# An encoder layer on one core: the FFN norm's factors on its rows instead of on the gate/up weights, other row pairs turned on TensorE, p evictions by load

## The chip, the cores and the metric

One NeuronCore of a Trainium2 chip runs one program. The metric is the device time of one execution in microseconds, from the first to the last instruction with what lies around it, and the median of several runs of a kernel. Engines: PE is TensorE's matmul, PEld its weight load, DVE is VectorE, ACT is ScalarE, POOL is GpSimd, SP issues the DMAs.

## The reference

One layer over x (2048 rows of 1024) mixes the rows with a gated delta net and an RG-LRU, and then computes the FFN and the per-layer embedding; the parts around the change are these:

```python
r = r + jnp.concatenate([dn_out, lru_out], axis=-1) @ w_out[i]
h2 = rmsnorm(r, norm2_g[i])            # r * rsqrt(mean(r*r) + eps) * norm2_g
gate = dwconv(h2 @ ffn_wg[i], ffn_conv_w[i], FFN_CONV_LEFT) + ffn_conv_b[i]
r = r + (jax.nn.gelu(gate) * (h2 @ ffn_wu[i])) @ ffn_wd[i]
pg = jax.nn.sigmoid(rmsnorm(r, ple_norm_g[i]) @ ple_wg[i] + ple_bg[i])
r = r + pg * (p[i] @ ple_wp[i])
return rmsnorm(r, final_g)
```

Everything is float32; D is 1024, D_FF 2816 (22 blocks of 128), and the FFN's convolution has three taps along the rows.

## The kernel before

**Numbers.** Each float32 operand of a large product is split into two float16 parts, high and low, by a ScalarE copy to float16 and a VectorE subtraction (split, L1668: copies L1673 and L1677, subtractions L1675 and L1679), and a product is the sum of three float16 products. Before a split, an operand is scaled by a power of two, worked out from the sum of its squares: ScalarE squares with an accumulated sum, one matmul with a matrix of ones adds over the partitions (for the gate/up weights L1859), and pow2_scale (L391) makes the scale and its inverse in six small VectorE steps.

**The FFN's products** use Strassen's scheme with seven products instead of eight over two halves each of rows, inner dimension and columns. operands (L1681) makes the seven operands of a side from four blocks: three are blocks themselves, four are sums or differences that GpSimd makes in place (L1702). product (L1706) issues one of the seven products in the matmuls of L1723, twelve of 512 columns each for a gate/up product. Products share banks: product 6 adds to the bank of product 1 and starts only after that was evicted (AFTER). gu_unit (L1884) is one unit: a gate (even n) or an up (odd n) projection of two column blocks for half of the rows (u is 0 or 1). units (L1727) interleaves two units in the order 1, 3 and 7 of the last, 2, 5, 4 of the last, 6. Products 1, 6, 5, 4 are evicted by ScalarE (L1927), products 2, 3, 7 by a VectorE addition (L1932). room (L1907) says which buffer an eviction must wait for: in an up projection with u = 1 it is the one that the first gate tile's convolution frees.

**One turn of the FFN** is a j from 0 to 10, four units. Beside the products stand: pair_weights (L1823), which loads the weights of a projection to come, multiplies them in place by norm2_g on GpSimd (L1851), squares them (L1854, summed at L1856), and splits their seven operands; gate_tile (L1963), which waits for the gate's products and for the act buffers, and makes tap scales (L1974), the middle tap on ScalarE (L1977), two side taps on VectorE (L1979, L1981) and the gelu (L1985); mult (L1988), which multiplies by the up projection on GpSimd (L1995); and act_post (L2000), which squares, scales and splits the result into seven operands, in sums of 128x1024 on GpSimd (L1702), stores them in DRAM and frees the act buffers for the next turn's gate_tile.

**The FFN norm.** norm_pairs (L1750) takes the rows in eight pairs of 128-row tiles, as the second output projection (out_lru, matmuls in L452, additions to r in L1580) finishes them in the order of TILES. Of each pair it squares the rows (L1769), makes the inverse root on VectorE, copies the rows times this factor on ScalarE into hv (L1777), stores r in DRAM (L1781), and makes the seven right operands. Pairs 0, 2, 4, 6 make and split them and turn the halves with seven DMA transposes (L1805); pairs 1, 3, 5, 7 turn the four blocks first, with 16 TensorE transposes (turned, L635) and four ScalarE evictions (L1794), and split into place. Pairs 0 to 3 serve the units with u = 0, pairs 4 to 7 those with u = 1.

**p.** p_products (L2384) multiplies p by ple_wp between FFN and down projection (matmuls in L452). Its post evicts the half m = 1 of each tile on VectorE (L2401) and m = 0 on ScalarE (L2404).

**What sets the order.** No engine's queue is ordered by the chip: a planner in the kernel (Sched, L158) runs before compilation. Each stream of work is a Python generator that yields steps with a modelled cost per engine (st), waits for named events (W) and takes memory from one arena (M). run (L250) always issues the step that can start earliest by the model, plus 20 ns for each unit of its stream's priority (PR, L53; a small number goes first), and memory is given in order of priority. So each changed cost, step or priority can move instructions anywhere behind it. S.t holds the modelled time up to which each engine is taken.

Of the kernel before, what the change touches and what calls it, by code (L numbers as in the profile page):

```python
# [25 lines left out]
PAGE = 4 * KB  # L26
SPOT, LX, LD = 0, 0, 0
AFTER_SUM = 5000
# [23 lines left out]
PARTS = (0, 1)  # L52
PR = {'main': 6, 'quarter': 5, 'build': 0, 'ring': 3, 'wo': 2, 'last': 0, 'norm': 2, 'lx': 2, 'conv': 2, 'dn': 2, 'prep': 2, 'chain': 6, 'z': 3, 'post': 2, 'lru': 1, 'lruout': 4, 'op': 2, 'pw': 3, 'evac': 0, 'cat': 5}  # L53

# [297 lines left out]
class Kern:  # L352
# [172 lines left out]
    def wprep(self, key, src, nk, n, gain, place, pieces=1, after=None, fold=False):  # L525
# [50 lines left out]
        if pieces > 1:  # L576
            yield st(dve=80)
            nc.vector.tensor_reduce(sm[:, 0:1], sm[:, 8 : 8 + (nk if fold else pieces)], axis=AX.X, op=ALU.add)
            tot = sm[:, 0:1]
        b = yield st(pe=20, bank=1, lag=SPOT)  # L580
        spot = self.bank(b)[:, 0:1]
# [429 lines left out]
    def head_post(self, h, which, G):  # L1011
# [45 lines left out]
        if which == "k":  # L1057
            bufs = yield M(2 * KB, 2 * KB)
            for q in range(4):
                sl = av[:, q * 512 : q * 512 + 512].rearrange("p (t n) -> p t n", t=4)  # L1060
                yield st(dve=c_tt(512))
                nc.vector.tensor_tensor(sl, sl, st_[:, 16 + 4 * q : 20 + 4 * q, None].to_broadcast([128, 4, 128]), op=ALU.mult)
                yield ahead(730)
                nc.sync.dma_start(dst[:, 4 * q : 4 * q + 4, 2], sl)
                b = yield st(pe=4 * 110, bank=1)
                P = self.bank(b)
                for i in range(4):
                    nc.tensor.transpose(P[:, i * 128 : i * 128 + 128], sl[:, i], c["ident"])
                kt = bufs[q % 2]
                yield st(act=c_act(512))  # L1070
                nc.scalar.activation(kt.f32(512), P, AF.Copy)
                S.release(b)
                yield st(dma=730)
                nc.sync.dma_start(dst[:, 4 * q : 4 * q + 4, 0], kt.f32(4, 128))
            for x in bufs:
                x.free()
# [673 lines left out]
    def norm_pairs(self):  # L1750


        nc, S = self.nc, self.S
        yield W("r", TILES[0], 1)
        sb = yield M(*[2 * KB] * 4, high=True)
# [3 lines left out]
        def begin(i):  # L1759
# [15 lines left out]
            for k, t in enumerate(ts):  # L1775
                yield st(act=c_act(D, 1))
                nc.scalar.activation(hv[:, k], self.rt(t), AF.Copy, scale=y[:, k : k + 1])  # L1777
            smb.free()
# [9 lines left out]
            v = [hv[:, k, z * 512 : z * 512 + 512] for z in range(2) for k in range(2)]  # L1788
            if i % 2:
                for x in v:  # L1790
                    b = yield st(pe=4 * 160, bank=1)
                    P = self.turned(x, b)
                    yield st(act=c_act(512))
                    nc.scalar.activation(x, P, AF.Copy)  # L1794
                    S.release(b)

            def put(n, x):
                if i % 2:
                    to = self.hU[u][n].f16(8, 512)[:, :, o : o + 128]
                    yield from self.split(x.rearrange("p (a n) -> p a n", n=128), to[:, 0:4], to[:, 4:8], 512)  # L1800
                    return
# [12 lines left out]
            if not left[0]:  # L1814
                S.fire("h2", 1)
                for x in sb:
                    x.free()
# [5 lines left out]
    def pair_weights(self):  # L1823
# [3 lines left out]
        for n in range(22):  # L1827
# [21 lines left out]
            for i in range(2):  # L1849
                yield st(pool=c_pool(1024) * 0.8)  # L1850
                nc.gpsimd.tensor_tensor(v[i], v[i], c["g2"][:, :, None].to_broadcast([128, KT, 128]), op=ALU.mult)  # L1851
            for i in range(2):
                yield st(act=c_act(1024))
                nc.scalar.activation(self.junk.b16(KT, 128), v[i], AF.Square, accum_out=sm[:, 8 + i : 9 + i])  # L1854
# [5 lines left out]
            yield from self.pow2_scale(spot, 1, 16384.0, w.s, w.inv, sm[:, 4:6])  # L1860
            S.release(b)
            blocks = [v[i][:, z * 4 : z * 4 + 4] for i in range(2) for z in range(2)]

# [520 lines left out]
    def p_products(self):  # L2384
# [12 lines left out]
        def post(t, m, b):  # L2397
            j, u = yield from ring.take()
            if m:
                yield st(dve=c_stt(512))  # L2400
# [228 lines left out]
    def go(self):  # L2629
# [13 lines left out]
        S.spawn(self.setup(), 0)  # L2643
        g1, g2 = (lambda: c["g1"]), (lambda: c["g2"])
        base = dict(k=4, q=0, v=8, z=12, lx=16, lg=20)
# [19 lines left out]
PACK = [  # L2665
    ("g1", 8), ("g2", 8), ("g3", 8), ("qkvw", 48), ("lxw", 16), ("lxb", 4), ("ba", 8), ("bx", 8),
    ("lam", 8), ("gl", 4), ("gd", 4), ("alog", 8), ("dtb", 8), ("fcw", 66), ("fcb", 22),
# [3 lines left out]
    "x", "p", "pack", "w_in", "w_ba", "w_gate", "w_out", "w_gu", "w_d", "ple_wg", "ple_wp",  # L2671
    "ple_bg", "final_g",
]


def lay_out(a):
# [13 lines left out]
    def all_rows(v):  # L2690
        return np.broadcast_to(np.asarray(v).reshape(1, -1), (128, np.asarray(v).size))

    parts = dict(
        g1=flat(rows(a["norm1_g"][0])), g2=flat(rows(a["norm2_g"][0])), g3=flat(rows(a["ple_norm_g"][0])),
        qkvw=flat(rows(a["dn_conv_w"][0]).transpose(0, 2, 1)), lxw=flat(rows(a["lru_conv_w"][0]).transpose(0, 2, 1)),
# [15 lines left out]
    for i, n in enumerate(("lru_wa", "lru_wx")):  # L2711
# [10 lines left out]
        ple_wg=np.asarray(a["ple_wg"])[0], ple_wp=np.asarray(a["ple_wp"])[0],  # L2722
        ple_bg=np.asarray(a["ple_bg"]), final_g=np.asarray(a["final_g"]).reshape(1, D),
    )

# [46 lines left out]
```

## Time and profile before

| | us |
|---|---|
| median of 3 runs (lowest, highest) | 2797.17 (2789.87, 2801.34) |
| the profiled execution | 2788.9 |
| its span, first to last instruction | 2787.2 |
| TensorE busy in the span | 2575.5 |
| VectorE, ScalarE, GpSimd busy | 1858.1, 1490.4, 928.3 |
| mean granted clock of TensorE | 0.973 |

Busy times count an engine's instructions from start to end. A row of a timeline gives the start, the length and the line of a run of like instructions, with the idle time before it and what ended it in brackets. A row of waits gives who waited for whom: in total, how often, and the longest. The granted clock is a share of full speed.

### The profile page before, as it was taken

To read this page: it belongs to the slowest core of one execution; us is meant where nothing else is said; L and a number is where in the kernel's file an instruction comes from. 1 tells how busy PE (TensorE), PEld (TensorE's weight loads), DVE (VectorE), ACT (ScalarE), POOL (GpSimd) and SP (SyncE) were. 2 spreads that over 40 slices of the span, in tenths; PEclk is the share of its full clock that TensorE was granted. 3 is DMA by queue.
4 is the path that set the end of the run, shared out by engine and by line. 5 is a ranking of instruction groups with operands and counts; after the bars stand their busy time and mean duration, and the time that the engine had idled before them with its cause. 6 is when DMAs were issued, how large, how long until landed. Compare 5 with 4: busy or idle time off the path is not lost. (4 is left out here: it accounts for less than half of the span.)

```text
span 2787.2 us, 40376 instructions
## 1 busy us (share of the span) xinstructions
PE 2575.5 (92%) x14072; PEld 1313.2 (47%) x14072; DVE 1858.1 (67%) x3861; ACT 1490.4 (53%) x3120; POOL 928.3 (33%) x662
## 2 busy tenths in 40 slices
PE   7998997999889989988999999999997799999998
PEld 4454453556565665443444444444443344444443
DVE  8668967976885667587666767776668842222458
ACT  6576767575657764366565665665656510101323
POOL 1133534745230000135555556555555500000000
PEclk9999999999999999998999999999999999999999
DMA  5232252366453477564222233323326754457973
GB/s 193 72 102 61 67 142 67 94 189 204 129 168 116 126 256 260 131 170 103 87 87 90 71 92 102 99 84 102 102 59 198 258 179 144 160 166 226 275 188 143
DMA packets 433452, 387.68 MB, mean 139 GB/s; under 512 B 158688, under 2 KB 362464, under 8 KB 433248
## 3 DMA queue, kind: packets, MB, share of 16 engines
q1 hardware_dynamic: 433248, 385.10, 46.6%
q8 instruction: 111, 1.82, 0.3%
q14 instruction: 93, 0.76, 0.1%
HBM read 229.82 MB, written 128.97 MB: 129 GB/s over the span
## 5 line engine op out<-in xcount | busy, mean ns | idle before, releaser
L1723 PE MATMUL P<-arena 128*128 128x512 f16 x5166 | 1139.4, 383 | 41.3 <-ACT arena L1927 39.7
L452 PE MATMUL P<-arena 128*128 128x512 f16 x4224 | 988.6, 385 | 26.2 <-DVE arena L2401 9.3
L1723 PEld LDWEIGHTS <-arena 128*128 128x128 f16 x5166 | 509.9, 99 | 659.9 <-issue 68.3
L452 PEld LDWEIGHTS <-arena 128*128 128x128 f16 x4224 | 414.5, 100 | 482.5 <-issue 48.0
L1702 POOL TENSOR_TENSOR arena<-arena 128x512 f32<-128x512 f32 (+1 forms) x200 | 373.5, 1872 | 357.7 <-DVE arena L1679 254.7
L1679 DVE SCALAR_TENSOR_TENSOR arena<-arena 128x512 f16<-128x512 f32 (+2 forms) x408 | 433.1, 1099 | 76.1 <-ACT arena L1677 75.1
L1677 ACT ACTIVATE arena<-arena 128x512 f16<-128x512 f32 (+2 forms) x408 | 281.4, 722 | 261.0 <-POOL arena L1702 127.3
L2186 DVE SCALAR_TENSOR_TENSOR arena<-P,arena 128x512 f32<-128x512 f32 x95 | 70.2, 749 | 214.7 <-PE P L1723 189.1
L1995 POOL TENSOR_TENSOR arena<-arena 128x512 f32<-128x512 f32 x88 | 129.1, 1486 | 128.4 <-ACT arena L1985 81.6
L1932 DVE TENSOR_TENSOR arena<-P,arena 128x512 f32<-128x512 f32 x132 | 90.6, 687 | 117.3 <-PE P L1723 115.0
L1851 POOL TENSOR_TENSOR arena<-arena 128x1024 f32<-128x1024 f32 x44 | 91.9, 2091 | 200.6 <-DMA arena<-in_w_gu_dram 200.6
L1927 ACT ACTIVATE arena<-P 128x512 f32<-128x512 f32 x176 | 102.5, 589 | 97.8 <-PE P L1723 91.8
L734 DVE SCALAR_TENSOR_TENSOR arena<-P,arena 128x511 f32<-128x511 f32 (+1 forms) x192 | 140.5, 742 | 1.9
L2237 ACT ACTIVATE arena<-arena 128x1024 bf16<-128x1024 f32 x16 | 16.9, 1057 | 231.9 <-DVE arena L2186 222.1
L1257 POOL TENSOR_TENSOR arena<-arena 128x512 f32<-128x512 f32 x64 | 118.3, 1866 | 57.7 <-DVE arena L1207 45.8
L553 POOL TENSOR_TENSOR arena<-arena 128x1024 f32<-128x1024 f32 (+1 forms) x25 | 52.1, 2090 | 195.8 <-DMA arena<-in_w_in_dram 195.7
L1455 ACT ACTIVATE arena<-P,arena 128x128 f32<-128x128 f32 x128 | 46.8, 365 | 98.7 <-PE P L1449 64.7
L1466 DVE SCALAR_TENSOR_TENSOR arena<-arena,P 128x128 f32<-128x128 f32 x128 | 43.7, 343 | 54.0 <-PE P L1461 19.9
L2110 ACT ACTIVATE arena<-arena 128x256 bf16<-128x256 f32 x88 | 35.9, 408 | 77.2 <-DMA arena<-in_w_d_dram 76.9
L1460 PE MATMUL P<-arena 128*128 128x128 f32 x256 | 60.3, 318 | 18.0 <-ACT arena L1458 9.6
L1160 POOL TENSOR_TENSOR arena<-arena 128x512 f32<-128x512 f32 x32 | 41.0, 1280 | 104.6 <-DVE arena L1157 95.9
L1444 DVE SCALAR_TENSOR_TENSOR arena<-P,arena 128x128 f32<-128x128 f32 x128 | 44.3, 347 | 44.3 <-PE P L1442 42.9
(240 smaller groups left out, 3487.1 us busy)
## 6 DMA issues: line engine op xcount, KB each, us to landing
arena<-hd SPq DMA_DIRECT2D x160, 256.0 KB, 3.3
actd<-arena SPq DMA_DIRECT2D x148, 256.0 KB, 2.6
arena<-actd SPq DMA_DIRECT2D x49, 640.0 KB, 4.0
arena<-in_w_gu_dram SPq DMA_DIRECT2D x44, 512.0 KB, 4.3
arena<-in_x_dram SPq DMA_DIRECT2D x32, 512.0 KB, 7.1
at<-arena SPq DMA_DIRECT2D x64, 256.0 KB, 2.8
arena<-at SPq DMA_DIRECT2D x128, 128.0 KB, 3.3
rd<-arena SPq DMA_DIRECT2D x32, 512.0 KB, 3.3
```

What stands on the lines that cost most here:

```text
L452: self.nc.tensor.matmul(out, l, r, start=(i + j == 0), stop=(i + j == m - 1))
L734: nc.vector.scalar_tensor_tensor(a[:, lo:hi], P[:, lo - sh : hi - sh], tp[:, j : j + 1], a[:, lo:hi], op0=ALU.mult, op1=ALU.add)
L1257: nc.gpsimd.tensor_tensor(pv[:, i % 2], a(slice(2 * i, 2 * i + 2)), b(slice(2 * i, 2 * i + 2)), op=ALU.mult)
L1677: nc.scalar.activation(hi, x, AF.Copy, scale=scale)
L1679: nc.vector.scalar_tensor_tensor(lo, x, scale, hi, op0=ALU.mult, op1=ALU.subtract)
L1702: nc.gpsimd.tensor_tensor(v[at], v[p], v[q], op=ALU.add if plus else ALU.subtract)
L1723: self.nc.tensor.matmul(out, l, r, start=(p in (1, 2, 5) and i + j == 0), stop=(p in (2, 3, 4) and i + j == m - 1), skip_group_check=True)
L1851: nc.gpsimd.tensor_tensor(v[i], v[i], c["g2"][:, :, None].to_broadcast([128, KT, 128]), op=ALU.mult)
L1927: nc.scalar.activation(d, P, AF.Copy)
L1932: nc.vector.tensor_tensor(d, P, d, op=ALU.add)
L1995: nc.gpsimd.tensor_tensor(v, v, U.buf.f32(2, 2, 4, 128)[:, i, s], op=ALU.mult)
L2186: nc.vector.scalar_tensor_tensor(v, self.bank(b), self.dsm[:, at : at + 1], v, op0=ALU.mult, op1=ALU.add)
```

## The change

The gain norm2_g leaves the gate/up weights: pair_weights no longer multiplies them on GpSimd. Instead norm_pairs loads norm2_g once as a row over all partitions, scales it by a power of two, and each row of hv is made by one VectorE instruction that multiplies by the row's factor and by that row; the scale's inverse goes into the weights' inverse scale. TensorE turns the pairs 4 to 7 instead of 1, 3, 5 and 7. The eviction of p's products goes to VectorE when the planner has VectorE free earlier than ScalarE, and else to ScalarE. The priority numbers of 'lx' and 'wo' rise from 2 to 4 and from 2 to 3. The lags that are written in (SPOT, KL, H2L) are all 0. norm2_g leaves the packed constants and becomes an input of its own.

```diff
-PR = {'main': 6, 'quarter': 5, 'build': 0, 'ring': 3, 'wo': 2, 'last': 0, 'norm': 2, 'lx': 2, 'conv': 2, 'dn': 2, 'prep': 2, 'chain': 6, 'z': 3, 'post': 2, 'lru': 1, 'lruout': 4, 'op': 2, 'pw': 3, 'evac': 0, 'cat': 5}
+PR = {'main': 6, 'quarter': 5, 'build': 0, 'ring': 3, 'wo': 3, 'last': 0, 'norm': 2, 'lx': 4, 'conv': 2, 'dn': 2, 'prep': 2, 'chain': 6, 'z': 3, 'post': 2, 'lru': 1, 'lruout': 4, 'op': 2, 'pw': 3, 'evac': 0, 'cat': 5}
...
     def norm_pairs(self):
...
+        (gb,) = yield M(4 * KB)
+        g = gb.f32(D)
+        yield st(dma=1456)
+        nc.sync.dma_start(g, self.io["norm2_g"].partition_broadcast(128))
+        gs = self.A.alloc(64).f32(16)
+        self.ginv = gs[:, 2:3]
+        yield st(act=c_act(D))
+        nc.scalar.activation(self.junk.b16(D), g, AF.Square, accum_out=gs[:, 0:1])
+        yield from self.pow2_scale(gs[:, 0:1], 1, 1.0, gs[:, 1:2], self.ginv, gs[:, 4:6])
+        yield st(dve=c_tt(D))
+        nc.vector.tensor_scalar(g, g, gs[:, 1:2], None, op0=ALU.mult)
+        S.fire("g2")
         yield W("r", TILES[0], 1)
...
             for k, t in enumerate(ts):
-                yield st(act=c_act(D, 1))
-                nc.scalar.activation(hv[:, k], self.rt(t), AF.Copy, scale=y[:, k : k + 1])
+                yield st(dve=c_stt(D))
+                nc.vector.scalar_tensor_tensor(hv[:, k], self.rt(t), y[:, k : k + 1], g, op0=ALU.mult, op1=ALU.mult)
...
-            if i % 2:
+            if i >= 4:
                 for x in v:
-                    b = yield st(pe=4 * 160, bank=1)
+                    b = yield st(pe=4 * 160, bank=1, lag=H2L)
                     P = self.turned(x, b)
...
             def put(n, x):
-                if i % 2:
+                if i >= 4:
...
-                for x in sb:
+                for x in sb + [gb]:
                     x.free()
...
     def pair_weights(self):
...
-            for i in range(2):
-                yield st(pool=c_pool(1024) * 0.8)
-                nc.gpsimd.tensor_tensor(v[i], v[i], c["g2"][:, :, None].to_broadcast([128, KT, 128]), op=ALU.mult)
             for i in range(2):
                 yield st(act=c_act(1024))
                 nc.scalar.activation(self.junk.b16(KT, 128), v[i], AF.Square, accum_out=sm[:, 8 + i : 9 + i])
...
             yield from self.pow2_scale(spot, 1, 16384.0, w.s, w.inv, sm[:, 4:6])
             S.release(b)
+            yield W("g2")
+            yield st(dve=75)
+            nc.vector.tensor_tensor(w.inv, w.inv, self.ginv, op=ALU.mult)
...
     def p_products(self):
...
         def post(t, m, b):
             j, u = yield from ring.take()
-            if m:
+            if S.t["dve"] < S.t["act"]:
                 yield st(dve=c_stt(512))
...
```

## Rows read from the trace of the kernel before

**Rows 1.** Stretches: PE, PEld, DVE, ACT, POOL busy; clock; DMA share; GB/s.

```profile
0.00:1130.00 1130.00, 1022.04 (x6971) 608.72 (x6972) 835.91 (x2210) 734.42 (x1835) 336.96 (x330) 0.97 0.47 141
1130.00:1300.00 170.00, 142.74 (x656) 68.04 (x655) 126.39 (x267) 94.22 (x166) 65.70 (x41) 0.92 0.59 141
...
1480.00:2090.00 610.00, 582.61 (x2664) 263.80 (x2662) 421.03 (x534) 367.85 (x653) 346.81 (x187) 0.98 0.29 89
2090.00:2250.00 160.00, 125.99 (x528) 53.69 (x527) 127.34 (x146) 85.16 (x125) 78.59 (x48) 0.91 0.66 211
```

**Rows 2.** Waits of PE, 1480 to 2100 us: total, times, longest.

```profile
PE P L1723 <- ACT arena L1927: 27.4, 8, 3.4
```

**Rows 3.** Timeline of PE, 1300 to 2260 us: start, length, line, [idle before].

```profile
1563.27 24.73 PE L1723 MATMUL P<-arena 128*128 128x512 f16 x106 [3.42 <-ACT arena L1927]
...
1623.07 14.84 PE L1723 MATMUL P<-arena 128*128 128x512 f16 x68
...
1797.46 23.04 PE L1723 MATMUL P<-arena 128*128 128x512 f16 x106 [3.43 <-ACT arena L1927]
```

**Rows 4.** Stretch right behind the wait; columns as in rows 1.

```profile
1563.27:1567.00 3.73, 3.73 (x10) 1.41 (x10) 3.73 (x4) 3.73 (x3) 1.42 (x1) 0.54 0.00 0
```

**Rows 5.** Timeline of DVE in that turn.

```profile
1627.59 0.69 DVE L1932 TENSOR_TENSOR arena<-P,arena 128x512 f32<-128x512 f32 x1 [0.67 <-PE P L1723]
1628.20 0.35 DVE L1974 TENSOR_SCALAR arena<-arena 128x3 f32<-128x3 f32 x2
...
1630.79 6.54 DVE L1979 SCALAR_TENSOR_TENSOR arena<-arena 128x2047 f32<-128x2047 f32 x2
```

**Rows 6.** Timeline of ACT in that turn.

```profile
1638.48 0.72 ACT L1677 ACTIVATE arena<-arena 128x512 f16<-128x512 f32 x1 [2.55 <-POOL arena L1702]
...
1640.69 1.08 ACT L1927 ACTIVATE arena<-P 128x512 f32<-128x512 f32 x2 [0.61 <-DVE arena L1981]
```

**Rows 7.** Timeline of POOL in that turn.

```profile
1605.34 2.35 POOL L1702 TENSOR_TENSOR arena<-arena 128x1024 f32<-128x1024 f32 x1 [4.82 <-DVE arena L1679]
1607.64 1.90 POOL L1851 TENSOR_TENSOR arena<-arena 128x1024 f32<-128x1024 f32 x1
...
1611.80 2.36 POOL L1851 TENSOR_TENSOR arena<-arena 128x1024 f32<-128x1024 f32 x1
1614.12 5.56 POOL L1702 TENSOR_TENSOR arena<-arena 128x1024 f32<-128x1024 f32 x2
1629.28 9.17 POOL L1702 TENSOR_TENSOR arena<-arena 128x512 f32<-128x512 f32 x4 [9.60 <-DVE arena L1679]
```

**Rows 8.** Single lines: times run, duration ns min/median/max, forms.

```profile
L1777 ACT ACTIVATE arena<-arena x16: 1131/1140/1150, 1174.1 to 1260.5; 128x1024 f32<-128x1024 f32 x16
...
L2518 DVE SCALAR_TENSOR_TENSOR arena<-arena x16: 1275/1284/1286, 2709.6 to 2782.2; 128x1024 f32<-128x1024 f32 x16
...
L1805 SPq DMA_TRANSPOSE arena<-arena x28: 1232/1276/2403, 1180.4 to 1276.8; - x28
...
L1856 DVE TENSOR_TENSOR arena<-arena x22: 148/160/2312, 1155.9 to 2050.4; 128x1 f32<-128x1 f32 x22
...
L1702 POOL TENSOR_TENSOR arena<-arena x200: 1261/1680/3195, 1167.2 to 2234.9; 128x512 f32<-128x512 f32 x80, 128x1024 f32<-128x1024 f32 x20
...
L2401 DVE TENSOR_SCALAR arena<-P,arena x16: 727/740/751, 2145.0 to 2206.0; 128x512 f32<-128x512 f32 x16
```

**Rows 9.** Waits of PE, 1130 to 1300 us.

```profile
PE P L635 <- ACT arena L1777: 17.8, 4, 10.0
```

**Rows 10.** Timeline of PE around the FFN norm.

```profile
1222.42 1.12 PE L635 MATMUL P<-arena 128*128 128x128 f32 x4 [5.85 <-ACT arena L1777]
...
1263.49 2.77 PE L1723 MATMUL P<-arena 128*128 128x512 f16 x6
```

**Rows 11.** Waits of PE, 2090 to 2250 us.

```profile
PE P L452 <- DVE arena L2401: 9.3, 2, 6.8
...
PE P L452 <- ACT arena L2404: 3.9, 4, 1.3
```

More of the change, by code (lines that the diff above doesn't have):

```diff
@@ L26 @@
 PAGE = 4 * KB
-SPOT, LX, LD = 0, 0, 0
+SPOT = 0
+KL = 0
+H2L = 0
+LX, LD = 0, 0
 AFTER_SUM = 5000
@@ L579, in wprep @@
             tot = sm[:, 0:1]
-        b = yield st(pe=20, bank=1, lag=SPOT)
+        b = yield st(pe=20, bank=1, lag=SPOT if ("xT", 3) in S.ev else 0)
         spot = self.bank(b)[:, 0:1]
@@ L1064, in head_post @@
                 nc.sync.dma_start(dst[:, 4 * q : 4 * q + 4, 2], sl)
-                b = yield st(pe=4 * 110, bank=1)
+                b = yield st(pe=4 * 110, bank=1, lag=KL)
                 P = self.bank(b)
@@ L2643, in go @@
         S.spawn(self.setup(), 0)
-        g1, g2 = (lambda: c["g1"]), (lambda: c["g2"])
         base = dict(k=4, q=0, v=8, z=12, lx=16, lg=20)
@@ L2665 @@
 PACK = [
-    ("g1", 8), ("g2", 8), ("g3", 8), ("qkvw", 48), ("lxw", 16), ("lxb", 4), ("ba", 8), ("bx", 8),
+    ("g1", 8), ("g3", 8), ("qkvw", 48), ("lxw", 16), ("lxb", 4), ("ba", 8), ("bx", 8),
     ("lam", 8), ("gl", 4), ("gd", 4), ("alog", 8), ("dtb", 8), ("fcw", 66), ("fcb", 22),
@@ L2671 @@
     "x", "p", "pack", "w_in", "w_ba", "w_gate", "w_out", "w_gu", "w_d", "ple_wg", "ple_wp",
-    "ple_bg", "final_g",
+    "ple_bg", "final_g", "norm2_g",
 ]
@@ L2693, in lay_out @@
     parts = dict(
-        g1=flat(rows(a["norm1_g"][0])), g2=flat(rows(a["norm2_g"][0])), g3=flat(rows(a["ple_norm_g"][0])),
+        g1=flat(rows(a["norm1_g"][0])), g3=flat(rows(a["ple_norm_g"][0])),
         qkvw=flat(rows(a["dn_conv_w"][0]).transpose(0, 2, 1)), lxw=flat(rows(a["lru_conv_w"][0]).transpose(0, 2, 1)),
@@ L2723, in lay_out @@
         ple_bg=np.asarray(a["ple_bg"]), final_g=np.asarray(a["final_g"]).reshape(1, D),
+        norm2_g=np.asarray(a["norm2_g"])[0].reshape(1, D),
     )
```

## The prediction

> **What bounds the kernel now.** I read the stretches first. Of the span, 108 us of idle TensorE lie in the mixer half up to 1130 us, 27 us in the 170 us in which the second output projection ends and the FFN norm runs, 27 us in the steady part of the FFN (1480 to 2090 us) and 34 us in the 160 us between FFN and down projection [rows 1]; TensorE is the busiest engine in each, and its matmuls are not changed, so only these idle times, and the clock, can be won. In the steady FFN a single wait makes all of it: a matmul of the FFN's products waits for the ScalarE eviction of L1927, eight times, 27.4 us together [rows 2]. TensorE's timeline shows the shape: a wait of 3.42 us behind 68 matmuls, in every turn of 78 us (the waits at 1563.27 and 1797.46 are three turns apart, 234.19 us) [rows 3]. Behind the wait the granted clock is 0.54 over 3.7 us, near the lower of its two levels, 1.2 GHz [rows 4]. The 106 matmuls that follow take 24.73 us; behind the wait at 1797.46, where the clock did not fall, 23.04 [rows 3]. So the clock costs 1.69 us more, in seven of the eight turns, and a turn without the wait would be 5.1 us shorter.
>
> Who is late there? The matmul belongs to product 6 of the up projection's second unit. It adds to the bank of product 1, and ScalarE must evict product 1 first, into the buffer that the gate's convolution of the same turn gives free (room, L1907). The timelines of VectorE and ScalarE give the chain: tap scales L1974 at 1628.20, the middle taps on ScalarE, the side taps L1979 from 1630.79 (two, 6.54 us), L1981, and then the eviction at 1640.69 [rows 5, 6]. TensorE had been standing since 1637.91 (1623.07 + 14.84) [rows 3]. The gate's products were done long before; gate_tile starts its taps only when act_post of the turn before has made its operands and so freed the act buffers. Those depend on four GpSimd sums of 128x1024 (L1702), which GpSimd does in order with two multiplications of the next gate/up weights by norm2_g (L1851) between them, from 1605.34 to 1619.68 [rows 7].
>
> **The change, part by part.** The sum is made against the profiled execution: 2788.9 us, its span 2787.2. The median of the runs shown, 2797.17, stands 8.3 us above it; I carry that difference over.
>
> The 44 multiplications L1851 go. Two of each turn's four lie inside the chain just told: 1.90 + 2.36 = 4.26 us [rows 7], more than the 3.42 that TensorE waits. I take the eight waits as gone: 27.4 us [rows 2] and 7 x 1.69 = 11.8 us of clock [rows 3], 39 us. It cannot be more, since the matmuls stay; at the other end it is nothing gained (what it could lose is the second rival). Next late would be ScalarE's in-order queue: a split of the next weights (L1677 at 1638.48) waited 2.55 us for GpSimd's sums and ended at 1639.20 [rows 6]. An eviction written behind it would still leave TensorE some 2 us of its wait. But that split's scale also comes about 4 us earlier now, because the weights' squares no longer wait for L1851, so I expect it out of the way; half the gain is the price if not.
>
> The FFN norm's rows: 16 ScalarE copies of 1.14 us go, and 16 VectorE multiplications by the row's factor and the g row come. The same form, 128x1024 with a second SBUF input, takes 1.284 us in the last stage [rows 8]. VectorE gets 20.5 us, ScalarE loses 18.2. VectorE is busy for 126 of the stage's 170 us [rows 1], so this is not covered everywhere: eight of the 16, 10.3 us, belong to the last four pairs, and I count 9 us of them as lengthening the way to the first FFN product. Against it, pairs 1 and 3 are no longer turned on TensorE in the midst of the projection: of its waits for their copies, 17.8 us, the last pair's was 10.0 [rows 9], and the other 7.8 us, which stood in front of projection matmuls, go, I count 7. The pairs 4 and 6 are turned in their place, with the same 16 transposes and four evictions a pair, and pair 6's now come after the projection: TensorE has nothing else to do there. The 14 DMA transposes of pairs 4 and 6 move forward to pairs 1 and 3, 1.28 us of SP each [rows 8], 17.9 us; behind them on the in-order SP queue stand the last transposes for the projection and the stores of r. Pair 3's rows are there at about 1222 us, and seven transposes are 9 us, well before the first FFN product at 1263.49 [rows 10]: nothing. Net 2 us lost; the bounds are 18 us gained (all 17.8) and 22 us lost (all 20.5 on the path, and some clock).
>
> Here a rule speaks against the change. The trace shows what GpSimd does to VectorE: the sum of 128x1 at L1856 takes 0.16 us, but up to 2.31 while GpSimd is at work [rows 8]. The Trainium skill ("SBUF — State Buffer", section "Who interferes with whom") says that a VectorE instruction with two SBUF inputs and a GpSimd instruction that reads SBUF exclude each other for the whole instruction; the new multiplications are of that kind, the ScalarE copies were not. By that rule the norm's term would be that of the third rival, by the row of L2518 alone it is the 2 us above.
>
> The g row is prepared before the first pair (one DMA of 512 KB, a Square, seven small VectorE steps, one scaling): nothing; were it late, the first pair would be, by less than 5 us. Its 4 KB of the arena can delay another buffer through the norm, which is in the bound of 22. The wait for g in pair_weights is over before the second pair of weights is loaded; 22 multiplications of 128x1 at 0.16 us, like L1856 [rows 8], hide behind the taps: nothing, or by L1856's longest, 2 us a turn.
>
> The p evictions: now 16 on VectorE (L2401, 0.74 us each [rows 8]) and 16 on ScalarE. VectorE is busy for 127 of the 160 us there, ScalarE for 85 [rows 1], and TensorE waits 9.3 us for the former and 3.9 for the latter [rows 11]. The load rule will give ScalarE more. I count half of the 9.3, 5 us gained; bounds 13 gained (both) and 4 lost (the ScalarE wait doubled).
>
> The priorities of the lx and output-weight streams (2 to 4, 2 to 3) move the written-out order of the mixer half, which has 108 us of idle TensorE in many small waits [rows 1]. No row says which way: nothing, with 12 us to either side, a ninth of it.
>
> Sum: -39 + 2 - 5 + 0 = -42; 2788.9 - 42 = 2747 in a profiled execution, 2755 as a median.
>
> **The rivals.** First: the tap chain is not moved. The order of each queue is fixed before the run by a model of costs, and L1974 stands on VectorE right behind the addition L1932, done at 1627.59, which follows TensorE [rows 5]. If the plan keeps that place, the change doesn't do for the FFN what the shorter GpSimd queue offers; 2 us lost in the norm and 5 won in p remain: 2794. Against it: the model counts the multiplications too, and sees the chain 4 us shorter.
>
> Second, slower: the sums of the next weights are written ahead of act_post's. Its place is the GpSimd queue between 1605 and 1620 us of each turn. The weights are ready earlier now; their four sums take 5.0 us by L1702's shortest (4 x 1.261) [rows 8], 9.17 in the profile beside the taps [rows 7]. It decides from the point at which they precede the last of act_post's sums: then the chain gains 4.26 and loses 5.0 to 9.17, 0.8 to 4.9 us a turn, over nine turns 7 to 44 us. With the 3 us won elsewhere: 2801 to 2838, in the middle 2820. Against it: they need the old operands' buffers free, which TensorE's products set.
>
> Third: the norm pays the lock. 16 x (1.284 + 1.68, the median of L1702 [rows 8]) = 47 us of VectorE instead of 20.5; with half of it behind the last four pairs, the way is 24 us longer instead of 9: 15 us of the gain go, 2770, and 2793 if all of it is on the path.
>
> **How the numbers follow.** A measurement of this kernel can tell about 0.5%, 14 us, from no change. My forecast has 0.60: 2755, by itself 2733 to 2780 (half the FFN's gain lost, or the norm and the mixer at their better ends). The first rival has 0.17, the second 0.13, the third 0.10. Faster (below 2783) are the forecast nearly whole, a fifth of the first and two thirds of the third: 0.69. Slower (above 2811) are the second, mostly, and the far ends of the first: 0.16. Within: 0.15. The range for 8 in 10 runs from 2727 to 2808; it takes in the first and third rivals and leaves out the upper half of the second.
>
> **What will show it.** Right: four L1702 sums of 128x1024 with nothing between, 9.4 to 11 us; L1974 some 4 us earlier in a turn; less than 8 us of waits for L1927 from 1480 to 2100; turns of 73 us. In the norm, new VectorE instructions of 1.28 us, or above 2 us for the third rival. Wrong: turns of 78 us or more, or a mixer half that ends over 12 us away from 1130 us.

## The result and the profile after

The changed kernel takes 2759.67 us (median of 4 runs, 2757.07 to 2763.62), the kernel before beside it 2796.41 (4 runs): ratio 0.9871, 95% interval 0.9848 to 0.9895. The profiled execution took 2759.3 us with a span of 2757.4, 29.8 less than the span before. The medians differ by 36.7: the profiled execution of before was 7.5 below its median, that of after 0.4.

The stretches of the changed kernel, columns as in [rows 1]; the FFN is cut at 2060 us here, since it ends earlier:

```profile
1130.00:1300.00 170.00, 140.48 (x653) 66.89 (x652) 140.00 (x280) 77.19 (x147) 56.75 (x36) 0.90 0.56 144
1480.00:2060.00 580.00, 580.00 (x2711) 265.58 (x2710) 420.91 (x553) 372.92 (x658) 276.34 (x156) 1.00 0.32 96
2060.00:2220.00 160.00, 123.42 (x525) 52.46 (x524) 123.33 (x137) 85.45 (x124) 76.81 (x48) 0.93 0.64 201
```

In the steady FFN TensorE is busy for all of the 580 us at a granted clock of 1.00. In the norm's 170 us it has 29.5 us idle, VectorE's busy time has risen to 140.00.

TensorE's waits of the changed kernel from 1290 to 2250 us, which answer to [rows 2] and [rows 11]:

```profile
PE P L456 <- ACT arena L2421: 10.1, 5, 4.5
PE P L1727 <- ACT arena L1944: 9.8, 2, 6.2
PE P L456 <- DVE arena L2418: 5.0, 2, 3.0
```

Lines have moved: L1727 is the FFN's matmul (L1723 before), L1944 the ScalarE eviction (L1927), L1949 VectorE's addition (L1932), L1991 the tap scales (L1974), L1994 the middle tap, L1996 and L1998 the side taps (L1979, L1981), L1706 the GpSimd sums (L1702), L1683 and L1681 the splits, L2418 and L2421 the p evictions on VectorE and ScalarE. The eight waits for the eviction are gone; of the FFN's two that are left one lies in the second turn and one in the last. In p the wait for VectorE has halved and that for ScalarE grown.

One turn of the changed kernel, first from VectorE's timeline, to be held against [rows 5] (start, duration, instruction, count, in brackets the idle time before it and what ended it):

```profile
1620.10 0.68 DVE L1949 TENSOR_TENSOR arena<-P,arena 128x512 f32<-128x512 f32 x1
...
1624.34 0.36 DVE L1991 TENSOR_SCALAR arena<-arena 128x3 f32<-128x3 f32 x2
1626.52 0.69 DVE L1949 TENSOR_TENSOR arena<-P,arena 128x512 f32<-128x512 f32 x1 [1.82 <-PE P L1727]
1627.99 2.35 DVE L1996 SCALAR_TENSOR_TENSOR arena<-arena 128x2047 f32<-128x2047 f32 x1 [0.78 <-ACT arena L1994]
...
1630.86 2.34 DVE L1998 SCALAR_TENSOR_TENSOR arena<-arena 128x2047 f32<-128x2047 f32 x1
```

From ScalarE's timeline of the same turn, the eviction, to be held against [rows 6]:

```profile
1633.55 0.58 ACT L1944 ACTIVATE arena<-P 128x512 f32<-128x512 f32 x1
```

From GpSimd's timeline of the same turn, to be held against [rows 7]:

```profile
1602.74 16.89 POOL L1706 TENSOR_TENSOR arena<-arena 128x512 f32<-128x512 f32 x8 [18.09 <-DVE arena L1683]
```

The tap scales L1991 stand *ahead* of the addition L1949 that waits for TensorE, by 2.18 us. Before, L1974 stood right *behind* that addition, 0.61 us after its start [rows 5]. Also, VectorE now does the two side taps of the first gate one after the other; before it did L1979 for both gates first, and then L1981 for both:

```profile
1637.25 5.61 DVE L1981 SCALAR_TENSOR_TENSOR arena<-arena 128x2047 f32<-128x2047 f32 x2
```

The eviction needs the first gate's two only: they end at 1633.20, 8.86 us after L1991 started. Before, the first of these two L1981 took 3.35 us and ended at 1640.60, 12.40 us after L1974. So two things moved together in VectorE's queue: the chain starts 2.79 us earlier against the addition, and it is 3.54 us shorter. The wait was 3.43. GpSimd makes eight sums in one run, four of the next weights and four of act_post, which alternate in its queue (the row prints the form of the first; every second one is 128x1024).

For the accounts below I cut every profiled execution at the same instructions: the end of the wait for catl, an operand of the second output projection that comes back from DRAM (the projection's start, 1150.86 us before, 1156.49 after), the first tap scale, that of the second turn, that of the tenth, and the end. "Eight turns" is from the second to the tenth. Each ratio is to runs of before taken beside it, whose medians lay between 2795.21 and 2796.94. In before and e1, whose queues have the same order but for the multiplications, no stretch differs by more than 1.3 us.

| kernel | median, us | ratio to before | projection to first tap | to second turn | eight turns | to the end |
|---|---|---|---|---|---|---|
| before | 2796.41 | 1 | 156.4 | 90.2 | 619.4 | 770.4 |
| after | 2759.67 | 0.9871 | 154.4 | 94.4 | 582.8 | 769.4 |
| e1, before without the instruction | 2795.51 | 0.9998 | 157.7 | 90.3 | 619.5 | 771.2 |
| e6, and without its cost | 2763.79 | 0.9881 | 152.9 | 91.8 | 585.9 | 774.5 |
| e9, before, last pairs turned | 2775.78 | 0.9927 | 158.2 | 104.4 | 581.7 | 778.4 |
| e5, before, act_post first | 2813.93 | 1.0061 | 157.6 | 87.2 | 637.6 | 774.1 |
| e2, after, multiplied, planned | 2779.55 | 0.9949 | 154.2 | 109.4 | 583.9 | 772.1 |
| e3, after, multiplied, unplanned | 2788.87 | 0.9974 | 157.4 | 97.2 | 602.9 | 772.3 |
| e4, after, blocks last | 2785.73 | 0.9967 | 153.2 | 103.2 | 582.0 | 787.4 |
| e10, after, rows on ScalarE | 2781.99 | 0.9946 | 154.0 | 91.9 | 585.6 | 791.4 |
| e11, after, odd pairs turned | 2766.78 | 0.9888 | 156.7 | 91.3 | 585.2 | 772.1 |
| e8, after, p by half | 2754.68 | 0.9849 | 154.7 | 94.3 | 580.9 | 767.4 |
| e7, after, act_post first | 2750.20 | 0.9830 | 155.4 | 92.2 | 579.9 | 765.7 |
| e12, e7 and e8 | 2752.97 | 0.9845 | 154.2 | 92.2 | 579.9 | 765.5 |

From before to after: eight turns -36.6, norm and first turn (-2.0 + 4.2) +2.2, the rest -1.0, and the stretch up to the projection +5.6, together -29.8. That last figure says nothing of the change: e1, whose queues have the order of before throughout, starts its projection at 1158.7 us, 7.8 later than before's profile.

### The profile page after: what moved, and what is told of

The parts are those of the page before. It is cut to its first block, busy times and chain, and to the rows that moved or that the text cites. A ratio compares the mean times of both kernels' runs of the same rounds, so it can differ in the third digit from the quotient of the medians.

```text
span 2757.4 us, 40429 instructions
## 1 busy us (share of the span) xinstructions
PE 2561.9 (93%) x14072; PEld 1311.3 (48%) x14072; DVE 1867.5 (68%) x3902; ACT 1479.5 (54%) x3110; POOL 825.2 (30%) x618
## 4 chain that ended last, share of the span: by engine, by line
PE 53%; DVE 6%; DMA 1%; ACT 1%; issue 1%; POOL 0%; SPq 0%; DVEq 0%; ACTq 0%
PE P L1727 40%; PE P L456 12%; DVE arena L1683 2%; DVE arena L1679 1%; PE P L2301 1%; DVE arena L1794 1%; DVE arena L1584 0%; DMA ppd<-arena 0%; DMA arena<-in_w_d_dram 0%; DMA arena<-catl 0%; DMA arena<-actd 0%; ACT arena L1681 0%; POOL arena L1706 0%; PE P L1452 0%; DVE arena L2418 0%
## 5 line engine op out<-in xcount | busy, mean ns | idle before, releaser
L1727 PE MATMUL P<-arena 128*128 128x512 f16 x5166 | 1127.2, 380 | 15.7 <-ACT arena L1944 9.8
L456 PE MATMUL P<-arena 128*128 128x512 f16 x4224 | 983.6, 384 | 32.2 <-ACT arena L2421 10.1
L1727 PEld LDWEIGHTS <-arena 128*128 128x128 f16 x5166 | 507.1, 98 | 624.1 <-issue 25.6
L1683 DVE SCALAR_TENSOR_TENSOR arena<-arena 128x512 f16<-128x512 f32 (+2 forms) x408 | 449.5, 1133 | 118.6 <-ACT arena L1681 118.3
L1706 POOL TENSOR_TENSOR arena<-arena 128x512 f32<-128x512 f32 (+1 forms) x200 | 352.5, 1776 | 507.6 <-DVE arena L1683 358.4
L1681 ACT ACTIVATE arena<-arena 128x512 f16<-128x512 f32 (+2 forms) x408 | 283.0, 723 | 294.7 <-POOL arena L1706 139.8
L2203 DVE SCALAR_TENSOR_TENSOR arena<-P,arena 128x512 f32<-128x512 f32 x95 | 70.1, 750 | 225.9 <-PE P L1727 190.2
L2012 POOL TENSOR_TENSOR arena<-arena 128x512 f32<-128x512 f32 x88 | 136.3, 1569 | 241.2 <-ACT arena L2002 175.6
L1944 ACT ACTIVATE arena<-P 128x512 f32<-128x512 f32 x176 | 102.5, 587 | 80.7 <-PE P L1727 76.1
L1261 POOL TENSOR_TENSOR arena<-arena 128x512 f32<-128x512 f32 x64 | 118.4, 1865 | 58.8 <-DVE arena L1211 46.8
L1949 DVE TENSOR_TENSOR arena<-P,arena 128x512 f32<-128x512 f32 x132 | 90.3, 684 | 36.7 <-PE P L1727 36.6
L1164 POOL TENSOR_TENSOR arena<-arena 128x512 f32<-128x512 f32 x32 | 40.9, 1280 | 104.0 <-DVE arena L1161 96.7
L1584 DVE SCALAR_TENSOR_TENSOR arena<-P,arena 128x512 f32<-128x512 f32 x64 | 47.7, 747 | 29.8 <-PE P L456 29.6
L728 ACT ACTIVATE arena<-P,arena 128x512 f32<-128x512 f32 x64 | 44.9, 703 | 42.1 <-PE P L456 37.1
```

Source lines behind the costliest of these rows:

```text
L456: self.nc.tensor.matmul(out, l, r, start=(i + j == 0), stop=(i + j == m - 1))
L1261: nc.gpsimd.tensor_tensor(pv[:, i % 2], a(slice(2 * i, 2 * i + 2)), b(slice(2 * i, 2 * i + 2)), op=ALU.mult)
L1681: nc.scalar.activation(hi, x, AF.Copy, scale=scale)
L1683: nc.vector.scalar_tensor_tensor(lo, x, scale, hi, op0=ALU.mult, op1=ALU.subtract)
L1706: nc.gpsimd.tensor_tensor(v[at], v[p], v[q], op=ALU.add if plus else ALU.subtract)
L1727: self.nc.tensor.matmul(out, l, r, start=(p in (1, 2, 5) and i + j == 0), stop=(p in (2, 3, 4) and i + j == m - 1), skip_group_check=True)
```

## The experiments

The theories: **A**, the prediction's, that GpSimd's time for the two multiplications among act_post's sums made the eviction late; **B**, that the order of VectorE's queue around the tap chain did (the mechanism of the first rival).

**e1: the time away, the order kept.**

```diff
                 yield st(pool=c_pool(1024) * 0.8)
-                nc.gpsimd.tensor_tensor(v[i], v[i], c["g2"][:, :, None].to_broadcast([128, KT, 128]), op=ALU.mult)
```

> The kernel before, without the 44 GpSimd multiplications of L1851, but with their modelled cost still booked, so that every other queue keeps the order of before. It leaves out the factor norm2_g. Theory A, GpSimd's time is the cause: the two multiplications inside act_post's sums (1.90 + 2.36 us) made the eviction late, so the eight waits for it (27.4 us) and seven times 1.69 us of clock go, turns of 73 us, some 39 us less than before: ratio to before about 0.986. Rival B, the order is the cause (the first rival of the prediction): the order stays, so the waits stay; ratio 0.998 to 1.000.

Measured: ratio 0.9998 (0.9986 to 1.0010). One turn of e1 (its lines stand one lower than before's from the deleted line on), first GpSimd's timeline:

```profile
1614.68 10.38 POOL L1702 TENSOR_TENSOR arena<-arena 128x1024 f32<-128x1024 f32 x4 [4.82 <-DVE arena L1679]
```

VectorE's timeline of e1 behind it:

```profile
1636.93 0.69 DVE L1931 TENSOR_TENSOR arena<-P,arena 128x512 f32<-128x512 f32 x1 [0.67 <-PE P L1723]
1637.54 0.35 DVE L1973 TENSOR_SCALAR arena<-arena 128x3 f32<-128x3 f32 x2
...
1646.58 5.61 DVE L1980 SCALAR_TENSOR_TENSOR arena<-arena 128x2047 f32<-128x2047 f32 x2
```

ScalarE's timeline of e1, the eviction:

```profile
1650.02 1.08 ACT L1926 ACTIVATE arena<-P 128x512 f32<-128x512 f32 x2 [0.61 <-DVE arena L1980]
```

And TensorE's timeline of e1, the matmul that waited for it:

```profile
1650.66 9.62 PE L1723 MATMUL P<-arena 128*128 128x512 f16 x36 [3.42 <-ACT arena L1926]
```

The four sums now stand with nothing between them, 10.38 us, the first sign that the prediction asked for, and nothing is won. From the addition to the eviction it is 1650.02 - 1636.93 = 13.09 us; before, 1640.69 - 1627.59 = 13.10 [rows 5, 6]. The chain hangs on the addition, the addition on TensorE. GpSimd's 4.26 us ahead of it were slack. Theory A falls. A rule of the Trainium skill fits this ("PSUM — Partial Sum Buffer", section "Engine vs sequencer instructions"): VectorE's queue is strictly first in, first out, so what stands behind a waiting instruction waits too; the two distances agree with it.

**e6: the modelled cost away too, the plan free.**

```diff
-            for i in range(2):
-                yield st(pool=c_pool(1024) * 0.8)
-                nc.gpsimd.tensor_tensor(v[i], v[i], c["g2"][:, :, None].to_broadcast([128, KT, 128]), op=ALU.mult)
```

> The kernel before without the 44 multiplications and without their modelled cost, nothing else changed (it leaves out the factor norm2_g). The plan is free to move, and in it L1974 stands one addition earlier than before, as in the changed kernel. Theory B: the waits of the steady FFN go, 2796 - 35, 2755 to 2764, so this part alone brings the changed kernel's gain, and the norm, the turned pairs and p together come to nothing. If it comes out below 2752, those other parts cost what is missing.

Measured: 0.9881 (0.9866 to 0.9896), eight turns in 585.9 us. Against e1 the only difference is what the planner believes, and it is worth 32 us. This part alone brings nearly the whole gain of the change.

**e9: another part alone, all multiplications in place.**

```diff
-            if i % 2:
+            if i >= 4:
```

(twice, in norm_pairs)

> The kernel before with one part of the change alone: TensorE turns the last four row pairs in place of every second one. All 44 multiplications and their modelled cost stay. In this plan L1974 stands one addition earlier from the third turn on, though GpSimd has all its work. Theory B (the order decides, and the plan has more than one order that it can settle in): from the third turn on no wait for L1927, turns of 73 us, as in e2; the second turn's taps stand one addition later, as in e2 and e4, where that turn was 9 to 15 us longer; 2765 to 2780. Theory A (GpSimd's work sets the waits): turns of 78 us, 2794 to 2800.

Measured: 0.9927 (0.9905 to 0.9949). One turn of e9, from VectorE's timeline:

```profile
1852.75 0.68 DVE L1932 TENSOR_TENSOR arena<-P,arena 128x512 f32<-128x512 f32 x1
...
1857.75 0.35 DVE L1974 TENSOR_SCALAR arena<-arena 128x3 f32<-128x3 f32 x2
1860.18 2.35 DVE L1979 SCALAR_TENSOR_TENSOR arena<-arena 128x2047 f32<-128x2047 f32 x1 [2.09 <-ACT arena L1977]
1862.45 0.68 DVE L1932 TENSOR_TENSOR arena<-P,arena 128x512 f32<-128x512 f32 x1
1863.05 3.38 DVE L1981 SCALAR_TENSOR_TENSOR arena<-arena 128x2047 f32<-128x2047 f32 x1
```

and from GpSimd's:

```profile
1823.45 3.75 POOL L1851 TENSOR_TENSOR arena<-arena 128x1024 f32<-128x1024 f32 x2 [4.16 <-DMA arena<-in_w_gu_dram]
...
1862.20 5.99 POOL L1851 TENSOR_TENSOR arena<-arena 128x1024 f32<-128x1024 f32 x2 [8.24 <-DMA arena<-in_w_gu_dram]
```

The multiplications are there, four a turn, and the eight turns take 581.7 us, as after. They stand in pairs outside act_post's sums, L1974 is ahead of the addition, and the first gate's side taps follow each other. The second of them takes 3.38 us beside the multiplications from 1862.20, and still they end 8.68 us after L1974. So the steady waits never needed GpSimd's work to go; another set of turned pairs, hundreds of microseconds earlier, puts the plan into the better order as well. The price is the second turn, 14.2 us longer than before, as in e2.

**e2 and e3: the multiplications put back into the changed kernel**, with their cost in the plan and without:

```diff
+            for i in range(2):
+                yield st(pool=c_pool(1024) * 0.8)
+                nc.gpsimd.tensor_tensor(v[i], v[i], c["ones"][:, 0:KT, None].to_broadcast([128, KT, 128]), op=ALU.mult)
             for i in range(2):
                 yield st(act=c_act(1024))
```

(e3 has no second line.)

> The changed kernel with the 44 GpSimd multiplications put back, by a factor of ones, and with their modelled cost, so the plan sees them as before. In this plan they do not stand between act_post's sums but two together, ahead of them. Theory A (what counts is work inside the chain from the product to the eviction): ahead of the sums GpSimd was idle for 18.09 us in a turn of the changed kernel, so 4.3 us there are covered; 0 to 12 us more than the changed kernel's 2760, no waits of 3.4 us in each turn. Rival C, GpSimd's load as such is the cause: the waits come back in each turn, 2790 to 2800.

> The changed kernel with the same 44 multiplications put back, but with no modelled cost: every other queue has exactly the order of the changed kernel, GpSimd has its 44 instructions more, ahead of act_post's sums. Theory A: covered by GpSimd's idle 18.09 us ahead of the sums; 2758 to 2772. Rival C (load): the chain of the taps comes 4.3 us later in each turn and the waits come back, 2790 to 2800.

Measured: e2 0.9949 (0.9932 to 0.9966), e3 0.9974 (0.9959 to 0.9988); both lie between what A and C expected. In e2 the steady turns are those of after (583.9 us), so load as such, C, is not it; 15 us are lost ahead of the second turn's taps (1421.75 in e2). TensorE's timeline of e2 (its lines stand three higher than after's there) has two long waits around them, first for the sum of the next weights' squares (L1873), which follow the multiplications, and then for the eviction:

```profile
1426.09 0.59 PE L1876 MATMUL P<-arena 128*128 128x1 f32 x2 [13.50 <-DVE arena L1873]
1435.48 4.75 PE L1727 MATMUL P<-arena 128*128 128x512 f16 x13 [8.80 <-ACT arena L1947]
```

In e3 (lines two higher than after's), whose other queues stand in the order of after, TensorE's waits from 1480 to 2060 us are:

```profile
PE P L1727 <- ACT arena L1946: 8.1, 5, 2.3
PE P L1727 <- DVE arena L1951: 5.0, 6, 1.5
```

ScalarE's timeline of e3 ahead of one of the longest (2.29 us, to 1663.60):

```profile
1661.38 1.06 ACT L1870 ACTIVATE arena<-arena 128x1024 bf16<-128x1024 f32 x1 [2.75 <-POOL arena L1867]
...
1662.98 0.58 ACT L1946 ACTIVATE arena<-P 128x512 f32<-128x512 f32 x1
```

The first gate's side taps had ended at 1659.59, but the eviction stands behind a square of the next weights (L1870), and that waited for its multiplication (L1867). The eight turns take 602.9, 20.1 longer than after. So once the order is good, GpSimd's time can count, in this turn by what stands ahead of the eviction in ScalarE's queue and not by the chain of theory A: work the plan doesn't know of makes waits of up to 2.3 us, and, known to the plan, the same work costs the steady turns 1.1 us in all.

**e5 and e7: one number for the order**, in before and in after:

```diff
-                        S.spawn(self.act_post(n // 2), 2)
+                        S.spawn(self.act_post(n // 2), -30)
```

> The kernel before with one number changed: act_post is spawned with priority -30 in place of 2, so the plan puts its instructions, and with them the tap chain, earlier. All 44 multiplications stay, the norm, the turned pairs and p stay. In this plan L1974 stands one addition of L1932 earlier in every turn, the last too. Theory B (the order of VectorE's queue set the waits): the eight waits and the 6.2 us of the last turn go; 2796 less 35 to 45, ratio 0.984 to 0.988. Theory A (GpSimd's time set them): the multiplications are all there, 2790 to 2797. Between, if the order moves the chain and GpSimd's time then binds as in e3 (2.4 us a turn): 2770 to 2778.

> The changed kernel with act_post spawned at priority -30. The steady turns keep their place, the taps of the second turn come one addition earlier. Theory B: the wait of 3.64 us at 1415 goes with some clock, the one of 6.21 us at 2080 stays; 3 to 6 us less than the changed kernel, 2754 to 2757. If act_post ahead of the weights' splits makes a product wait for its weights instead: 2765 or more.

Measured: e5 1.0061 (1.0046 to 1.0076), a miss on the other side; e7 0.9830 (0.9815 to 0.9845). TensorE's waits of e5 from 1480 to 2060 us:

```profile
PE P L1723 <- ACT arena L1677: 17.7, 14, 1.3
PE P L1723 <- DVE arena L1679: 15.3, 7, 2.2
PE P L1723 <- DVE arena L1932: 3.2, 2, 2.7
```

Not one wait for the eviction is left. e5 is also the one kernel whose steady turns (from the third on) have an early chain and still the old order of the side taps, L1979 for both gates first. In the turn at 1636.78, L1974 starts 20.4 us before the matmul that needs the eviction (the same one by its count in TensorE's queue); in before it was 9.7 us (1637.91 - 1628.20). So an early place can be enough. But TensorE is held up here by the other waits, and no run at its full pace has the early place without the new order of the side taps: how much of the gain belongs to which is not shown. The next weights' splits (L1677, L1679) now come late, and the eight turns take 18 us more than before. With act_post first, and multiplications between weights and splits, the weights are the next late. In the changed kernel, which has no multiplications, the same number gains: e7's second turn loses its wait of 3.64 us, which stands in TensorE's timeline of after,

```profile
1415.30 10.00 PE L1727 MATMUL P<-arena 128*128 128x512 f16 x32 [3.64 <-ACT arena L1944]
```

and its median is 9.5 below after's. The two were measured beside different runs of before; the intervals of their ratios (0.9815 to 0.9845, 0.9848 to 0.9895) just do not meet. By the medians e7 is the fastest kernel of this study.

**e4: the memory of the norm's last pair.** In the changed kernel the last pair's factors (L393) are ready long before VectorE uses them (L1794); VectorE's timeline of after shows it:

```profile
1254.26 0.16 DVE L393 SCALAR_TENSOR_TENSOR arena<-arena 128x2 f32<-128x2 f32 x1
...
1273.64 2.17 DVE L1794 SCALAR_TENSOR_TENSOR arena<-arena 128x1024 f32<-128x1024 f32 x1
...
1277.40 1.27 DVE L1794 SCALAR_TENSOR_TENSOR arena<-arena 128x1024 f32<-128x1024 f32 x1
```

TensorE's timeline of after, the transposes that waited for them:

```profile
1275.95 1.09 PE L639 MATMUL P<-arena 128*128 128x128 f32 x4 [14.83 <-DVE arena L1794]
1278.82 2.79 PE L639 MATMUL P<-arena 128*128 128x128 f32 x12 [1.78 <-DVE arena L1794]
```

```diff
         self.more(0)
+        yield W("last pair")
         self.blk = yield M(8 * KB, 8 * KB)
```

> The changed kernel, where the FFN takes its two 8 KB blocks only after the last row pair of the norm has its own 8 KB. Theory D (the memory is the cause of the norm's loss): the last pair's multiplications of L1794, which ran at 1273.6 and 1277.4 us though their factors were ready at 1254.4, come right behind the factors, and TensorE's wait of 14.8 us at 1275.95 shrinks to under 6 us; 5 to 10 us less than the changed kernel: about 2752. Rival E (VectorE's own load is the cause: it does 16 row multiplications more, and the last pair stands in its queue whatever the memory): the wait only moves, within 2 us of the changed kernel.

Measured: 0.9967 (0.9954 to 0.9981), 26 us slower than after. In e4's VectorE timeline the last pair's rows now follow its factors:

```profile
1252.30 0.16 DVE L393 SCALAR_TENSOR_TENSOR arena<-arena 128x2 f32<-128x2 f32 x1
1253.02 1.28 DVE L1794 SCALAR_TENSOR_TENSOR arena<-arena 128x1024 f32<-128x1024 f32 x1
```

So the memory did hold them back. But the stretch up to the second turn grew by 7.6 us (256.4 instead of 248.8), and no time was won. In the place of the 14.83 TensorE waits twice for the eviction L1944, the first time at the FFN's start and the second around the second turn's taps (1412.91):

```profile
1279.85 8.98 PE L1727 MATMUL P<-arena 128*128 128x512 f16 x28 [10.66 <-ACT arena L1944]
...
1422.91 27.26 PE L1727 MATMUL P<-arena 128*128 128x512 f16 x112 [10.69 <-ACT arena L1944]
```

And 18 us went in a stage that the edit doesn't touch, the last. TensorE's timeline of e4 there:

```profile
2659.80 111.25 PE L456 MATMUL P<-arena 128*128 128x512 f16 x504 [16.01 <-DVE arena L2517]
```

VectorE's timeline of e4 there (L2517 and L2523 are after's L2516 and L2522):

```profile
2604.45 1.41 DVE L2517 SCALAR_TENSOR_TENSOR arena<-P,arena 128x512 f32<-128x512 f32 x2
...
2655.26 0.69 DVE L2523 TENSOR_TENSOR arena<-arena 128x512 f32<-128x512 f32 x1 [18.87 <-DMA arena<-ppd]
```

VectorE's timeline of after at the same place:

```profile
2616.55 0.75 DVE L2516 SCALAR_TENSOR_TENSOR arena<-P,arena 128x512 f32<-128x512 f32 x1 [4.43 <-PE P L456]
...
2646.18 0.69 DVE L2522 TENSOR_TENSOR arena<-arena 128x512 f32<-128x512 f32 x1 [17.21 <-DMA arena<-ppd]
```

VectorE stands 17 to 19 us for the reload of p in both. In after it evicts a bank 12 us before it stops (at 2646.18 - 17.21 = 2628.97). In e4 it stops at 2636.39, the last evictions ahead of that began at 2604.45, and TensorE waits for the next one. e10 has the same wait:

```profile
PE P L456 <- DVE arena L2516: 16.2, 1, 16.2
```

**e10, e11 and e8: three parts of the change undone one by one.**

```diff
-                yield st(dve=c_stt(D))
-                nc.vector.scalar_tensor_tensor(hv[:, k], self.rt(t), y[:, k : k + 1], g, op0=ALU.mult, op1=ALU.mult)
+                yield st(act=c_act(D, 1))
+                nc.scalar.activation(hv[:, k], self.rt(t), AF.Copy, scale=y[:, k : k + 1])
```

> The changed kernel with the norm's rows made by ScalarE copies again, without the gain row (it leaves out the gain in the rows). The tap chains stand as in the changed kernel. The prediction had 9 us on the path for the 16 VectorE multiplications: then 2751. If the last pair's wait comes from the memory or from ScalarE's splits, or the time only moves to the next wait (as in e4): 2756 to 2762.

```diff
-            if i >= 4:
+            if i % 2:
```

> The changed kernel with every second row pair turned on TensorE again, as before. The tap chains stand as in the changed kernel. The prediction had 7 us gained by moving the turns out of the second output projection: then 2767. If what is gained there is given back at the last pairs, 2757 to 2762.

```diff
-            if S.t["dve"] < S.t["act"]:
+            if m:
```

> The changed kernel with the p evictions by the half m again instead of by load. The prediction had the load rule at 5 us gained: 2765. The trace of the changed kernel shows the waits for VectorE halved (9.3 to 5.0) and those for ScalarE grown (3.9 to 10.1): then the rule gains nothing, 2757 to 2762.

Measured: e10 0.9946 (0.9932 to 0.9961), a miss, because of the 16.2 us in the last stage; up to the second turn's taps it is 245.9 us against 248.8, so VectorE's rows cost 2.9 us there, twice the 1.4 by which before and e1 differ. e11 0.9888 (0.9868 to 0.9909), 7 us above after by the medians but with overlapping intervals; up to the second turn it is 248.0 against 248.8, so what it loses lies behind the norm (eight turns +2.4, the rest +2.7), not where the prediction put the 7 us. e8 0.9849 (0.9833 to 0.9865): 5 us below after by the medians, 2.0 in the stretch from the tenth turn to the end, intervals overlapping.

**e12: e7 and e8 together.**

> The changed kernel with act_post at priority -30 (e7) and the p evictions by the half m (e8). If the two add up, 2750 - 5 = 2745; if the p rule is worth nothing in this order (in e7 the stretch from the last turn's taps to the end was 683.2 us with the load rule, in e8 684.9 without it), 2749 to 2753.

Measured: 0.9845 (0.9827 to 0.9862), no better than e7. In that order the p rule is worth nothing that can be told.

## Why the prediction was right, and where not

The time was right: 2755 forecast, 2759.67 measured, inside 2733 to 2780. By terms:

- **The FFN, -39: the size was right (-36.6 in eight turns, turns of 72.9 us instead of 77.4), the reason wrong.** The step that failed is "Two of each turn's four lie inside the chain just told: 1.90 + 2.36 = 4.26 us [rows 7], more than the 3.42 that TensorE waits". I followed the chain by its data, from the sums to the taps, and took each link as binding. The rows had the answer: L1974 starts right at the end of an addition that had itself waited for TensorE [rows 5]. What is saved ahead of an instruction that waits for TensorE doesn't make it earlier; e1 took the 4.26 us away and won nothing (0.9998). What the runs show in its place is the order that the plan writes: with the same GpSimd work left out, e6 wins the waits and e1 doesn't. That the time came out was luck in this step: 39 us was what all the waits and their clock were worth, whatever took them away.
- **The first rival** had the mechanism right and only doubted that the plan would move. It moved, as the sentence against it said: the plan sees the chain without the multiplications. e6 shows that their modelled cost is enough for that, e9 that it isn't needed: with only other pairs turned the plan also falls into the better order, and in e2 it keeps it with the multiplications back. Which part moved it in the change itself can't be named, since either is enough.
- **The sign "four L1702 sums of 128x1024 with nothing between"** was the wrong one: after shows eight alternating sums in 16.89 us, without a wait; e1 shows the sign, without a gain. Every kernel that lost the eight waits of 3.4 us has L1974 one addition earlier in its steady turns, and all of them but e5 have the first gate's side taps one after the other there.
- **The second rival's** condition came true in part, since in after's GpSimd queue some of the next weights' sums precede the last of act_post's; its price was not paid: TensorE waits for nothing in these turns. Side taps of 2.35 us instead of 3.27 (half of 6.54 [rows 5]) came with it: in after those 9 us of sums no longer run beside them. The Trainium skill ("SBUF — State Buffer", section "Who interferes with whom") has such VectorE instructions and GpSimd's reads exclude each other; the rows agree in sign, 0.9 us a tap.
- **The norm, +2:** measured +0.8 (against e1) to +2.2 up to the second turn. Its two parts were both too large: the rows cost 2.9 us (e10), not 9, and the turned pairs gained nothing that e11 shows in that stretch, where 7 were counted. TensorE's longest wait there is still the last pair's, 14.83 us for VectorE where it was 10.0 for ScalarE [rows 9].
- **The third rival** fell: the 16 new instructions take 1.272 to 2.166 us, median 1.278, as the row of L2518 said [rows 8].
- **p, -5:** the step "The load rule will give ScalarE more. I count half of the 9.3" was right on the share (12 evictions on VectorE and 20 on ScalarE) and on the half (5.0 us of waits for VectorE), and it forgot the other side: waits for ScalarE rose from 3.9 to 10.1 [rows 11]. It also left out that other matmuls wait for these evictions (L2284 and L2134, 7.3 us before and 0.8 after) and for DMA (6.5 before and 12.8 after). From the tenth turn to the end 1.0 us was won, where before and e1 differ by 0.8.
- **The mixer half, 0:** right. TensorE's queue there has the same order in both kernels; the 5.6 us between the profiles are less than the 7.8 between before and e1.

## What to carry to other kernels

Before costing a chain at its slowest link, look at what stands directly ahead of each link in its own queue: if that waits for the very engine you want to feed, the link's place is the price, and its inputs have slack. Where a planner fixes the order, a change acts first through what the planner believes, and may settle in another order anywhere downstream, so test "work away, cost kept" and "cost away" apart. And a part that looks 20 us worse may only have met a wait three stages later: cut every trace at the same instructions before judging.

## What was not expected

The stretch up to the projection took from 1150.9 to 1166.4 us in these profiles, though TensorE's queue has the same order there in all of them. After and e3, whose queues are the same up to there, differ by 9.9, so a single profile can't tell an effect below some 10 us in it. VectorE's 17 to 19 us stop for the reload of p stands in after, e4 and e10 alike, and costs nothing or 16 us by how lately it had evicted a bank. In after SP issues the first of these reloads at 2641.89, behind eight pairs of DMA transposes that hold its queue from 2599.68 on, 3.6 to 5.1 us a pair.
